# Fewer stored weight operands, fewer partial sums and moved staging in a seven-product MLP

## The chip, the cores and the metric

One core of a Trainium2 chip runs the whole program. The metric is the device time of one execution in microseconds (us). Engines: TensorE (PE, its weight loads PEld), VectorE (DVE), ScalarE (ACT), GpSimd (POOL), and SyncE (SP), which here issues nearly all DMAs.

## The reference, cut to what matters

One layer of a recurrent decoder runs over 2048 prompt tokens and 32 sample tokens. Everything up to the first layer norm is the same before and after; the change lies in the MLP that follows it:

```python
x = layer_norm(ALPHA * x + g1 * mix, ln1_g, ln1_b)
h = x * (1.0 + sc2) + sh2                                   # (2080, 1024)
f = dot(square(relu(dot(h, mlp_w1) + mlp_b1)), mlp_w2) + mlp_b2   # 1024 -> 4096 -> 1024
x = layer_norm(ALPHA * x + g2 * f, ln2_g, ln2_b)
```

All of it is fp32. A product of two fp32 operands is made of three matmuls on fp32r operands: each operand is split into a high part (a copy on ACT) and a low part (operand minus high part, on DVE or POOL), and high*high, high*low and low*high are summed in PSUM.

## The kernel before

**Tiling.** The 2080 tokens are worked on in three groups of 692 to 696 (gidx 0, 1, 2), each in two halves of w = 348 or 346 tokens. The 4096 hidden features are worked on in 16 chunks (c) of 256. Four chunks make a block: four calls of `mlp1` (first matrix) and one call of `mlp2_seven` (second matrix, on two pairs of chunks). Group 2 leaves its last two chunks to plain products.

**Seven products.** Each 2x2 product of blocks takes seven block products (Strassen-Winograd) of the weight operands a11, a12, a22 (plain blocks) and s1 to s4 (sums of blocks) with token operands (b1, b2, t13, t42 in `mlp1`; b11 to b22 and t1 to t4 in `mlp2_seven`). One product is 12 matmuls in `mlp1` and 48 in `mlp2_seven`, so a half block (four `mlp1`, or one `mlp2_seven`) is 336 matmuls.

**PSUM.** In `mlp1`, a11, s2, s3 and a22 add up in one bank (`x`), read by ACT after each step (`s1`, `u2`, `u2` again, then the Relu). s1 (product P5) and s4 (product P3) have banks of their own, and DVE forms `u4` = P5 + u2 from them. Four banks are taken per call from the rotation `M1_BANKS`. In `mlp2_seven`, PRODUCTS says which products go on in the four shared banks `m2x` (True) and which get four banks of their own, and into which quarters of the accumulator `acc` each is added: s1 goes into two quarters, so a call makes 8 x 4 additions to `acc` (on DVE, the first ones of a group on ACT).

**Weights.** In group 0 the raw weights are loaded, combined on DVE, split into operands (`operand`, L763: one 128x1024 tile, high and low half), used, and all stored to DRAM (`W1d`, `W2d`, 512 KB each): 7 per chunk for the first matrix, 14 per pair of chunks for the second. Groups 1 and 2 load those stored operands (`kept`, L773) and split nothing. Group 0's operands live in a ring of 6 buffers (SLOTS), groups 1 and 2 use a ring of 15 (READY); two thirds of group 0's low parts are made by DVE, one third by POOL.

**Staging.** `stage_h` (L704) makes the token operands of a later group: it loads two rows of `Nd`, scales them on ACT, stores, sums them on DVE, and stores again (`Od`). All eight calls, four for group 1 and four for group 2, stand in group 0, after chunks 4 to 11. `conv_h` splits them at the end of a group.

**What sets the order.** A scheduler orders each engine's instructions when the program is built; each engine then runs its list in order. SP's list holds stores (waiting for a split) and loads in one queue. In groups 1 and 2 the layer norm of the group before (`ln2`) runs beside the products.

Of the kernel before, what the change touches and what calls it, by code (L numbers as in the profile page):

```python
# [35 lines left out]
def trunk(ctx: ExitStack, tc: tile.TileContext, *args):  # L36
# [741 lines left out]
    def order_of(gidx, c):  # L778

        if c:  # L780
            return "a11", "a12", "s2", "s1", "s3", "s4", "a22"
        return ("a11", "a12", "s4", "s2", "s1", "s3", "a22") if gidx else ("a11", "s2", "s1", "s3", "a22", "a12", "s4")

    def weights(gidx, c):

# [12 lines left out]
        for key in order_of(gidx, c):  # L798
# [246 lines left out]
    with lpool("p5") as p5_:  # L1045
# [93 lines left out]
        def mlp2_seven(gidx, c0, hids, steps=None):  # L1139
# [3 lines left out]
            pairs = []  # L1143
            for i in range(0, len(hids), 2):
                av = {}
                for key, c, h in () if gidx else (("a11", 0, 0), ("a21", 0, 1), ("a22", 1, 1), ("a12", 1, 0)):
                    t = stage[0](f"q{key}_{gidx}_{c0 + i}").rearrange("p (f d) -> p f d", f=2)
                    r0 = 2 * (c0 + i + c) * P
                    w_load(t, w2[r0:r0 + 2 * P, 512 * h:512 * h + 512].rearrange("(f p) d -> p f d", p=P))
                    av[key] = t  # L1150
# [36 lines left out]
            banks = None  # L1187
            for l, r, grows, to in PRODUCTS:
# [4 lines left out]
                fresh = not (grows and banks)  # L1193
                if not grows:
                    ps = [rot(M2_BANKS, f"m2{l}_{gidx}_{c0}_{b}")[:, :w] for b in range(4)]
                else:
                    if fresh:
                        banks = [ptile([P, 512], X_BANKS[b], f"m2x_{gidx}_{c0}_{b}")[:, :w] for b in range(4)]
                    ps = banks
# [156 lines left out]
        for gidx in range(3):  # L1356
            c0 = 0
            while c0 < NCK - 2 * (gidx == 2):
                hids = []
                for c in range(c0, min(c0 + 4, NCK - 2 * (gidx == 2))):  # L1360
# [525 lines left out]
```

## Time and profile before

| | us |
|---|---|
| three runs | 2157.93, 2162.76, 2165.63 |
| their median | 2162.76 |
| the profiled execution | 2165.93 |
| its span, first to last instruction | 2164.1 |
| PE busy in the span | 2038.4 |
| DVE, ACT, POOL busy | 1426.8, 1006.3, 489.7 |
| moved by DMA | 571.39 MB |

The page has 40 slices of 54 us each: about 14 for what comes ahead of the MLP, then group 0 (some 9 slices, to 1277 us), groups 1 and 2 (to 2107 us) and the end. "PE busy" counts an engine that has an instruction in flight. The views below are the busy times by stretch, the waits of PE's weight loads by what ended them, groups of instructions with mean durations, and a stretch of ACT's timeline.

### The profile page before, as it was taken

The numbers are of one execution on the slowest core, as the hardware profiler recorded it, in microseconds if no ns is written. First come the engines' busy times: TensorE is split into PE (matmuls) and PEld (weight loads), VectorE is DVE, ScalarE is ACT, GpSimd is POOL, SyncE is SP. The second block draws the span as 40 slices with busy tenths as digits, with TensorE's granted clock in tenths as the row PEclk, the third lists the DMA queues.
The fourth block names the chain that finished last, engine by engine and source line by source line (L and its number), as shares of the span: only waits on it lengthen the run. The fifth ranks groups of instructions, "written<-read, shape, count | busy, mean of one in ns | idle before, by whom it ended". The sixth has DMA issues, their size and how long they took to land.

```text
span 2164.1 us, 35479 instructions
## 1 busy us (share of the span) xinstructions
PE 2038.4 (94%) x13055; PEld 1915.4 (89%) x13055; DVE 1426.8 (66%) x2766; ACT 1006.3 (47%) x1923; POOL 489.7 (23%) x327
## 2 busy tenths in 40 slices
PE   7998999989999989889899899999999999999996
PEld 4987888888877789888899889999999999999996
DVE  5677897467887898688797854445444444554476
ACT  3446665546676456554645534333334343333342
POOL 2245323432433322121222401000002000001003
PEclk9999999999999989999999999999999999999998
DMA  9799765453342598999989899888889988898871
GB/s 334 162 267 266 220 192 171 134 149 83 103 110 79 181 325 315 397 341 369 348 325 351 312 365 370 306 282 297 304 293 332 383 302 303 286 310 293 278 271 53
DMA packets 367596, 571.39 MB, mean 264 GB/s; under 512 B 129451, under 2 KB 250703, under 8 KB 367423
## 3 DMA queue, kind: packets, MB, share of 16 engines
q1 hardware_dynamic: 363975, 567.84, 76.8%
q8 instruction: 103, 1.69, 0.3%
q10 hardware_dynamic: 3448, 1.29, 0.2%
q14 instruction: 70, 0.57, 0.1%
HBM read 388.10 MB, written 180.94 MB: 263 GB/s over the span
## 4 chain that ended last, share of the span: by engine, by line
PE 43%; DVE 4%; issue 3%; DMA 2%; POOL 0%; ACT 0%; SPq 0%; POOLq 0%; DVEq 0%; ACTq 0%
PE m1a L1072 15%; PE m2x L1211 11%; PE m1s L1072 6%; PE m2s L1211 6%; PE m2a L1211 3%; PE lt L1297 1%; DVE hw2s L44 1%; DVE acc L44 1%; DMA W1d<-w1s 0%; PE m L1247 0%; PE m L1248 0%; PE m L1249 0%; DVE hid L44 0%; DMA n<-Nd 0%; DVE lb L44 0%
## 5 line engine op out<-in xcount | busy, mean ns | idle before, releaser
L44 POOL TENSOR_TENSOR y<-y,ln_g 128x512 f32<-128x512 f32 (+3 forms) x28 | 37.6, 1360 | 636.7 <-ACT y L65 463.3
L65 ACT ACTIVATE ht<-hid 128x692 fp32r<-128x692 f32 (+1 forms) x92 | 72.1, 783 | 174.1 <-PE m2s L1211 62.8
L65 ACT ACTIVATE hid<-hid 128x346 f32<-128x346 f32 (+1 forms) x240 | 115.9, 491 | 72.3 <-DVE hid L62 63.5
L65 ACT ACTIVATE u<-m1a 128x346 f32<-128x346 f32 (+1 forms) x96 | 43.9, 458 | 188.5 <-PE m1a L1072 181.3
L44 DVE TENSOR_TENSOR lt<-hid,ht 128x692 fp32r<-128x692 f32 (+1 forms) x92 | 87.1, 947 | 64.8 <-ACT ht L65 64.5
L44 DVE TENSOR_TENSOR acc<-m2x,acc 128x346 f32<-128x346 f32 (+1 forms) x168 | 84.3, 513 | 61.4 <-PE m2x L1211 59.9
L62 DVE SCALAR_TENSOR_TENSOR hid<-m1s,vecB,u 128x346 f32<-128x346 f32 (+1 forms) x94 | 53.7, 576 | 97.3 <-ACT u L65 72.6
L44 DVE TENSOR_TENSOR hid<-hid,hid 128x692 f32<-128x692 f32 (+1 forms) x92 | 87.5, 951 | 35.0 <-ACT hid L65 34.9
L1211 PE MATMUL m2x<-ht,hw2s 128*128 128x348 f32 (+1 forms) x392 | 98.9, 329 | 5.3 <-DVE hw2s L44 5.3
L65 ACT ACTIVATE hb<-hid 128x692 fp32r<-128x692 f32 (+1 forms) x69 | 54.0, 784 | 98.7 <-PE m2x L1211 51.6
L44 DVE TENSOR_TENSOR lb<-hid,hb 128x692 fp32r<-128x692 f32 (+1 forms) x69 | 67.2, 974 | 17.6 <-ACT hb L65 17.4
L1211 PEld LDWEIGHTS m2x<-ht,hw2s 128*128 128x128 f32 x392 | 70.3, 194 | 6.6 <-DVE hw2s L44 6.6
L62 DVE SCALAR_TENSOR_TENSOR hid<-m1a,vecB,s 128x346 f32<-128x346 f32 (+1 forms) x48 | 27.6, 576 | 62.5 <-PE m1a L1072 57.5
L44 DVE TENSOR_TENSOR acc<-m2s,acc 128x346 f32<-128x346 f32 (+1 forms) x120 | 56.4, 509 | 13.9 <-PE m2s L1211 13.9
L1211 PE MATMUL m2x<-lt,hw2s 128*128 128x348 f32 (+1 forms) x196 | 63.5, 327 | 0.0
L1072 PE MATMUL m1s<-h2t13h,hw1s 128*128 128x348 f32 (+1 forms) x216 | 57.9, 330 | 4.9 <-DVE x L62 3.7
L44 DVE TENSOR_TENSOR u<-m1s,u 128x346 f32<-128x346 f32 (+1 forms) x48 | 24.8, 516 | 51.9 <-ACT u L65 30.3
L65 ACT ACT_TABLE_LOAD x40 | 51.3, 1283 | 16.0 <-DVE hgb L57 6.5
L1072 PE MATMUL m1a<-h2t42h,hw1a 128*128 128x348 f32 (+1 forms) x192 | 50.9, 328 | 5.8 <-ACT hw1a L65 2.4
L1072 PE MATMUL m1a<-h2t42h,hw1s 128*128 128x348 f32 (+1 forms) x184 | 51.1, 342 | 5.5 <-DVE hw1s L44 4.9
L1072 PE MATMUL m1a<-h2t13h,hw1s 128*128 128x348 f32 (+1 forms) x200 | 52.4, 325 | 2.3 <-ACT hw1s L65 1.7
L956 PE MATMUL op<-hwo,ybh 128*128 128x512 f32 x128 | 51.7, 407 | 2.9 <-ACT ybh L65 2.9
(820 smaller groups left out, 7763.1 us busy)
## 6 DMA issues: line engine op xcount, KB each, us to landing
W1d<-hw1s SPq DMA_DIRECT2D x53, 512.0 KB
W2d<-hw2s SPq DMA_DIRECT2D x53, 512.0 KB
hw1s<-W1d SPq DMA_DIRECT2D x44, 512.0 KB
hw2s<-W2d SPq DMA_DIRECT2D x44, 512.0 KB
lw1s<-W1d SPq DMA_DIRECT2D x42, 512.0 KB
w1s<-W1d SPq DMA_DIRECT2D x42, 512.0 KB
W2d<-hw2a SPq DMA_DIRECT2D x41, 512.0 KB
W1d<-hw1a SPq DMA_DIRECT2D x38, 512.0 KB
```

Source lines behind the costliest of these rows:

```text
L44: return eng.tensor_tensor(out=out, in0=in0, in1=in1, op=op)
L62: return V.scalar_tensor_tensor(out, in0, s, in1, op0, op1)
L65: return S.activation(out, in_, f, **kw).ins
L956: PE.matmul(ac[:w, :], yh[:, kk, o:o + w], wh[:, hs], start=(k == 0), stop=False)
L1072: PE.matmul(ps, x[:, k, :], h[:, k, o:o + w], start=(on is None and k + i == 0), stop=(k == 3 and i == 2), skip_group_check=on is not None)
L1211: PE.matmul(ps[2 * s_ + jj], x[:, f, js], h[:, f, :], start=(fresh and n + f + e == 0), stop=(n == len(pairs) - 1 and f + e == 3), skip_gr ...
L1297: PE.transpose(pt[:w, k * P:k * P + P], src[:, 4 * half + k, :], ident)
```

## The change

1. **mlp1:** s4 (P3) is added up in the bank of s1 (P5), after P5 was read; `u4` and its DVE addition go (one remains in the first chunk of groups 1 and 2, where it serves another purpose). Three banks per call instead of four. Except for the first chunk of groups 1 and 2, all chunks take the order a11, s2, s1, s3, a22, a12, s4.
2. **mlp2_seven:** s1 and s4 share four banks ("y"), a12 gets its own ("o") and comes first. s1 goes into one quarter, so 7 x 4 additions to `acc` are left.
3. **Storing:** group 0 stores s1 to s4 and a11 of the first matrix and s1 to s4 of the second; a12, a22 (first) and a11, a12, a22 (second) are not stored.
4. **Groups 1 and 2:** those plain blocks are loaded raw (one 512 KB load holds two operands) into the ring of 15 and split there, high part on ACT, low part on DVE (kind "c").
5. **Staging:** four calls stay in group 0 (chunks 3, 5, 7, 9, for group 1), four go to group 1 (same chunks, for group 2), with buffers of the ring of 15.

Counted over the program, ACT gets 154 instructions more, DVE 60 more (154 splits, less 46 + 48 additions), SP 157 fewer (80 stores and 77 loads); PE and POOL have as many as before.

```diff
-    W1d = dr.tile([16, 7, P, D], F32, tag="W1d", name="W1d")
-    W2d = dr.tile([8, 7, 2, P, D], F32, tag="W2d", name="W2d")
+    W1d = dr.tile([16, 5, P, D], F32, tag="W1d", name="W1d")
+    W2d = dr.tile([8, 4, 2, P, D], F32, tag="W2d", name="W2d")
...
-    KEYS = ("a11", "a12", "a22", "s1", "s2", "s3", "s4")
+    KEYS = ("s1", "s2", "s3", "s4", "a11")
...
-        low_turn[0] += 1
-        split(hi, lo, v, V if low_turn[0] % 3 else Q)
+        low_turn[0] += kind == "s"
+        split(hi, lo, v, V if kind == "c" or low_turn[0] % 3 else Q)
...
-        if c:
-            return "a11", "a12", "s2", "s1", "s3", "s4", "a22"
-        return ("a11", "a12", "s4", "s2", "s1", "s3", "a22") if gidx else ("a11", "s2", "s1", "s3", "a22", "a12", "s4")
+        if gidx and not c:
+            return "a11", "a12", "s4", "s2", "s1", "s3", "a22"
+        return "a11", "s2", "s1", "s3", "a22", "a12", "s4"
...
         if gidx:
-            return {key: kept(f"w1{key}_{nm}", W1d[c, KEYS.index(key)], 4) for key in order_of(gidx, c)}
+            t = f32(quad("c", f"rw1_{nm}")).rearrange("p (k c) -> p k c", k=4)
+            w_load(t, w1[512:D, c * 256:c * 256 + 256].rearrange("(k p) c -> p k c", p=P))
+            return {key: operand(f"w1{key}_{nm}", t[:, :, P:2 * P] if key == "a22" else t[:, :, 0:P], kind="c")
+                    if key in ("a12", "a22") else kept(f"w1{key}_{nm}", W1d[c, KEYS.index(key)], 4)
+                    for key in order_of(gidx, c)}
...
-            ops[key] = operand(f"w1{key}_{nm}", at[key], W1d[c, KEYS.index(key)])
+            ops[key] = operand(f"w1{key}_{nm}", at[key], W1d[c, KEYS.index(key)] if key in KEYS else None)
...
-        PRODUCTS = (("a11", "b11", True, (0,)), ("s1", "t1", False, (2, 3)), ("a12", "b21", False, (0,)),
-                    ("s2", "t2", True, (2,)), ("s4", "b22", False, (2,)), ("s3", "t3", True, (3,)),
-                    ("a22", "t4", True, (1,)))
+        PRODUCTS = (("a12", "b21", "o", (0,)), ("a11", "b11", "x", (0,)), ("s1", "t1", "y", (3,)),
+                    ("s2", "t2", "x", (2,)), ("s4", "b22", "y", (2,)), ("s3", "t3", "x", (3,)),
+                    ("a22", "t4", "x", (1,)))
...
                     p5_s = prod(key, "t13", 0)
-                    add(V, u4, p5_s, u2)
...
                 elif key == "s3":
                     prod(key, "t13", w, x)
-                    act(u2, x, AF.Copy)
-                    put(1, 1, p5_s, u2)
+                    act(u3, x, AF.Copy)
+                    put(1, 1, p5_s, u3)
                 elif key == "s4":
-                    ps = prod(key, "b2", w)
+                    ps = prod(key, "b2", w, p5_s)
...
-                        put(0, 1, ps, u4)
+                        put(0, 1, ps, u2)
...
+                sums_ = l[0] == "s"
+                if gidx and not sums_:
+                    for n, (nm, av, bv) in enumerate(pairs):
+                        av[l] = raw2(l, c0 + 2 * n, lambda t: f32(quad("c", t)))
...
-                        if gidx:
+                        if gidx and sums_:
                             wh, wl = kept(f"w2{l}{s_}_{nm}", at, 2)
                         else:
-                            wh, wl = operand(f"w2{l}{s_}_{nm}", av[l][:, :, 256 * s_:256 * s_ + 256], at)
+                            wh, wl = operand(f"w2{l}{s_}_{nm}", av[l][:, :, 256 * s_:256 * s_ + 256], at,
+                                             "c" if gidx else "s")
...
-        M1_BANKS, M2_BANKS, X_BANKS = "ADB", "CD", "ABAB"
+        M1_BANKS, M2_BANKS, X_BANKS = "ADB", "CDCD", "ABAB"
...
-        STAGE = range(4, 12)
+        STAGE = range(3, 11, 2)
...
-                    if not gidx and c in STAGE:
-                        i = STAGE.index(c)
-                        stage_h(1 + i // 4, i % 4, raw_tile)
+                    if gidx < 2 and c in STAGE:
+                        stage_h(gidx + 1, STAGE.index(c), (lambda nm: f32(quad("c", nm))) if gidx else raw_tile)
```

Three places in the engines' lists. In them `hw1a11_0_9` is the operand of weight block a11 of group 0, chunk 9, `rw1...` or `qa12...` a raw weight tile, `s1_`, `u2_`, `u3_` copies of the bank `x` (named `m1a11`), `hid` hidden values.

ACT in group 0, around chunk 9's operands, before:

```order
L65 ACTIVATE hw1a11_0_9_11393<-rw10_0_9_11389 128x512
L65 ACTIVATE hid1_0_8_11265<-hid1_0_8_11265 128x348 x2
L65 ACTIVATE hw1a12_0_9_11397<-lrw11_0_9_11391 128x512
L65 ACTIVATE hid0_0_8_11264<-m1a11_0_8_11269,vecB_250 128x348
L65 ACTIVATE nh2_1_1_11537<-nh2_1_1_11537,B1_5870,A1_5869 128x660
L65 ACTIVATE hid0_0_8_11264<-hid0_0_8_11264 128x348
L65 ACTIVATE nh2_2_0_11693<-nh2_2_0_11693,B1_5870,A1_5869 128x660
L65 ACTIVATE s1_0_9_11427<-m1a11_0_9_11430 128x348
L65 ACTIVATE hb11_0_8_11888<-hid0_0_8_11264 128x696
L65 ACTIVATE hw1s2_0_9_11403<-rw10_0_9_11389 128x512
L65 ACTIVATE w1s1_0_9_11407<-rw10_0_9_11389 128x512
L65 ACTIVATE u2_0_9_11428<-m1a11_0_9_11430 128x348
```

and after:

```order
L65 ACTIVATE hw1a11_0_9_11285<-rw10_0_9_11281 128x512
L65 ACTIVATE u2_0_8_11179<-m1a11_0_8_11181 128x348
L65 ACTIVATE hw1s2_0_9_11291<-rw10_0_9_11281 128x512
L65 ACTIVATE hw1s1_0_9_11295<-rw10_0_9_11281 128x512
L65 ACTIVATE u3_0_8_11180<-m1a11_0_8_11181 128x348
L65 ACTIVATE hw1a22_0_9_11304<-lrw11_0_9_11283 128x512
L65 ACTIVATE hid1_0_8_11177<-hid1_0_8_11177 128x348
L65 ACTIVATE s1_0_9_11317<-m1a11_0_9_11320 128x348
```

Before, the splits of chunk 9's s2 and s1 stand behind the copy of chunk 9's first product; after, they stand behind copies of chunk 8's, and two staging instructions (`nh2`) are gone from between.

ACT in group 1, around chunk 5, after:

```order
L65 ACTIVATE u2_1_5_14747<-m1a11_1_5_14749 128x346
L65 ACTIVATE y5_00_256_14990<-y5_00_256_14990,AB_5872,mods_78 128x92 x8
L65 ACTIVATE u3_1_5_14748<-m1a11_1_5_14749 128x346
L65 ACTIVATE hw1a22_1_7_15051<-lrw1_1_7_15041 128x512
L65 ACTIVATE hw1a12_1_7_15054<-lrw1_1_7_15041 128x512
L65 ACTIVATE hid1_1_5_14745<-hid1_1_5_14745 128x346
L65 ACTIVATE s1_1_6_14887<-m1a11_1_6_14890 128x346
```

Two splits of chunk 7 are new there, between two copies of chunk 5's and chunk 6's banks; before, no split stands in group 1's list outside `conv_h` and the hidden values' own.

SP in group 1, the loads of chunk 4's first-matrix weights, after:

```order
L757 DMA lrw1_1_4_14552<-in_mlp_w1_dram 128x4x256
L757 DMA hw1a11_1_4_14554<-W1d_71 128x1024
L757 DMA hw1s2_1_4_14556<-W1d_71 128x1024
L757 DMA hw1s1_1_4_14558<-W1d_71 128x1024
L757 DMA hw1s3_1_4_14560<-W1d_71 128x1024
L757 DMA lw1s4_1_4_14568<-W1d_71 128x1024
```

These are six loads where seven stood; the first is raw and has to be split into two operands.

## Rows read from the trace of the kernel before

**Rows 1.** The page: busy time, granted clock and DMA in 40 slices.

```profile
PE 2038.4 (94%) x13055; PEld 1915.4 (89%) x13055; DVE 1426.8 (66%) x2766; ACT 1006.3 (47%) x1923; POOL 489.7 (23%) x327
...
PEclk9999999999999989999999999999999999999998
DMA  9799765453342598999989899888889988898871
```

**Rows 2.** Busy time by stretch: group 0's half blocks, then groups 1 and 2.

```profile
core 0: us, PE busy (x) PEld busy (x) DVE busy (x) ACT busy (x) POOL busy (x), PEclk, DMA share, GB/s
756.00:826.00 70.00, 62.55 (x354) 59.57 (x353) 63.68 (x117) 36.44 (x72) 16.37 (x10) 0.90 0.90 324
826.00:879.30 53.30, 52.62 (x328) 51.73 (x326) 45.25 (x61) 32.95 (x59) 14.06 (x10) 1.00 0.89 335
879.30:950.00 70.70, 60.65 (x349) 56.45 (x349) 48.16 (x72) 38.22 (x73) 14.49 (x11) 0.98 1.01 380
950.00:1009.50 59.50, 56.99 (x338) 53.11 (x337) 56.60 (x88) 27.22 (x44) 12.74 (x9) 1.00 0.91 339
1009.50:1079.00 69.50, 59.84 (x338) 54.65 (x338) 46.37 (x79) 35.84 (x70) 12.96 (x10) 0.98 0.96 360
1079.00:1138.40 59.40, 56.11 (x338) 55.00 (x337) 56.18 (x82) 25.35 (x42) 14.92 (x10) 0.97 0.88 331
1138.40:1195.00 56.60, 53.63 (x329) 51.81 (x328) 41.43 (x60) 30.24 (x61) 11.94 (x9) 1.00 0.93 343
1195.00:1277.20 82.20, 70.89 (x407) 68.49 (x406) 64.93 (x81) 36.89 (x63) 29.63 (x17) 0.94 0.91 334
...
1323.00:2100.00 777.00, 776.58 (x4914) 774.79 (x4913) 379.80 (x736) 280.08 (x535) 71.39 (x54) 1.00 0.88 309
```

**Rows 3.** PE's weight loads, 879.3 to 1138.4 us: waited for, us, times, longest.

```profile
PEld m1a L1072 <- ACT hw1a L65: 6.7, 6, 1.4
PEld m1a L1072 <- DVE hw1s L44: 6.0, 4, 2.7
...
PEld m1a L1072 <- ACT u L65: 2.6, 3, 0.9
```

**Rows 4.** The same view, 1195 to 1277.2 us, then 1323 to 2100 us.

```profile
PEld m2s L1211 <- DVE hw2s L44: 5.5, 3, 2.7
...
PEld lt L1297 <- DVE y L62: 0.7, 1, 0.7
```

**Rows 5.** ACT's timeline in group 0: start, us, instruction, idle before and releaser.

```profile
1011.59 0.46 ACT L65 ACTIVATE s<-m1a 128x348 f32<-128x348 f32 x1 [7.21 <-PE m1a L1072]
1011.94 0.62 ACT L65 ACTIVATE hw1a<-lrw 128x512 fp32r<-128x512 f32 x1
1012.46 0.62 ACT L65 ACTIVATE hw1s<-rw 128x512 fp32r<-128x512 f32 x1
1019.31 0.46 ACT L65 ACTIVATE u<-m1a 128x348 f32<-128x348 f32 x1 [6.22 <-PE m1a L1072]
1019.66 0.62 ACT L65 ACTIVATE hw1s<-rw 128x512 fp32r<-128x512 f32 x1
```

**Rows 6.** DVE groups by shape, 879.3 to 1138.4 us: count, busy, mean ns, idle before.

```profile
L44 DVE TENSOR_TENSOR acc<-m2s,acc 128x348 f32<-128x348 f32 x24 | 11.3, 509 | 1.3 <-PE m2s L1211 1.3
L44 DVE TENSOR_TENSOR nh<-nh 128x346 f32<-128x346 f32 x15 | 9.8, 651 | 0.1
L44 DVE TENSOR_TENSOR nh<-nh,nh 128x346 f32<-128x346 f32 x14 | 7.6, 540 | 1.1 <-ACT nh L65 0.9
L44 DVE TENSOR_TENSOR hw1a<-lrw,hw1a 128x512 fp32r<-128x512 f32 x9 | 6.2, 686 | 2.2 <-ACT hw1a L65 2.2
L44 DVE TENSOR_TENSOR u<-m1s,u 128x348 f32<-128x348 f32 x8 | 4.2, 520 | 3.8 <-PE m1s L1072 2.5 <-ACT hw1a L65 1.3
```

**Rows 7.** DMAs: the staging's stores (880 to 1195 us); all packets of 879.3 to 1009.5 us.

```profile
Od<-nh SPq DMA_DIRECT2D x22, 346.0 KB
...
DMA packets 18738, 47.04 MB, mean 361 GB/s; under 512 B 1588, under 2 KB 6771, under 8 KB 18729
```

More of the change, by code (lines that the diff above doesn't have):

```diff
@@ L761, in both, with operand @@
         return [t[:, 512 * i:512 * i + 512].rearrange("p (a b) -> p a b", a=n) for i in range(2)]
-    def operand(nm, v, keep=None):
-        t = quad("s", nm)
+    def operand(nm, v, keep=None, kind="s"):
+        t = quad(kind, nm)
         hi, lo = both(t, v.shape[1])
-        low_turn[0] += 1
-        split(hi, lo, v, V if low_turn[0] % 3 else Q)
+        low_turn[0] += kind == "s"
+        split(hi, lo, v, V if kind == "c" or low_turn[0] % 3 else Q)
         if keep is not None:
@@ L1092, in put @@
                 square(v, SQA[2 * f + q])
-            s1, u2, u4 = vt("s1"), vt("u2"), vt("u4")
+            s1, u2, u3 = vt("s1"), vt("u2"), vt("u3")
             v01, v10 = hid[1][:, 0, :], hid[0][:, 1, :]
@@ L1107, in mlp1 @@
                     p5_s = prod(key, "t13", 0)
-                    add(V, u4, p5_s, u2)
                     if gidx and not c:
-                        add(V, v01, v01, u4)
+                        add(V, u2, p5_s, u2)
+                        add(V, v01, v01, u2)
                         square(v01, SQA[1])
@@ L1143, in mlp2_seven, with raw2 @@
             pairs = []
-            for i in range(0, len(hids), 2):
[L1145 to L1150, printed above, removed]
+            def raw2(key, cc, tile_):
+                c, h = {"a11": (0, 0), "a21": (0, 1), "a22": (1, 1), "a12": (1, 0)}[key]
+                t = tile_(f"q{key}_{gidx}_{cc}").rearrange("p (f d) -> p f d", f=2)
+                r0 = 2 * (cc + c) * P
+                w_load(t, w2[r0:r0 + 2 * P, 512 * h:512 * h + 512].rearrange("(f p) d -> p f d", p=P))
+                return t
+            for i in range(0, len(hids), 2):
+                av = {key: raw2(key, c0 + i, stage[0]) for key in (() if gidx else ("a11", "a21", "a22", "a12"))}
                 pairs.append((f"{gidx}_{c0 + i}", av, {"b11": hids[i][0], "b12": hids[i][1], "b21": hids[i + 1][0],
@@ L1186, in mlp2_seven @@
             taken = [c0 > 0] * 4
-            banks = None
-            for l, r, grows, to in PRODUCTS:
+            banks = {}
+            for l, r, total, to in PRODUCTS:
                 rs = []
@@ L1192, in mlp2_seven @@
                     rs.append(part(f"{r}_{nm}", bv[r]))
[L1193 to L1199, printed above, removed]
+                fresh = total not in banks
+                if fresh:
+                    banks[total] = [ptile([P, 512], (X_BANKS if total == "x" else M2_BANKS)[b],
+                                          f"m2{total}_{gidx}_{c0}_{b}")[:, :w] for b in range(4)]
+                ps = banks[total]
+                sums_ = l[0] == "s"
+                if gidx and not sums_:
+                    for n, (nm, av, bv) in enumerate(pairs):
+                        av[l] = raw2(l, c0 + 2 * n, lambda t: f32(quad("c", t)))
                 for s_ in range(2):
                     for n, ((nm, av, bv), (hh, hl)) in enumerate(zip(pairs, rs)):
-                        at = W2d[c0 // 2 + n, KEYS.index(l), s_]
-                        if gidx:
+                        at = W2d[c0 // 2 + n, KEYS.index(l), s_] if sums_ else None
+                        if gidx and sums_:
                             wh, wl = kept(f"w2{l}{s_}_{nm}", at, 2)
                         else:
-                            wh, wl = operand(f"w2{l}{s_}_{nm}", av[l][:, :, 256 * s_:256 * s_ + 256], at)
+                            wh, wl = operand(f"w2{l}{s_}_{nm}", av[l][:, :, 256 * s_:256 * s_ + 256], at,
+                                             "c" if gidx else "s")
                         for jj in range(2):
```

## The prediction, made before the result was known

> **What bounds the kernel now.** I read the page first, then a table of stretches, then the waits of PE's weight loads. The page [rows 1] shows PE busy 94% of the span and DMA near 9 tenths in most slices of the MLP, so any gain must come from a stretch in which PE waits. I cut the MLP at its half blocks [rows 2]: group 0's are A (756 to 826), B, C, D, E, F, G and H (1195 to 1277.2), in turn four `mlp1` calls and one `mlp2_seven` of 336 matmuls each. B takes 53.3 us with PE busy 52.6 of them; that is my measure of a half block at PE's own pace. Groups 1 and 2 run at that pace: in 1323 to 2100 PE is busy 776.58 of 777 us at full clock, DVE only 379.8 and ACT 280.1 [rows 2], and a weight load hardly ever waits there (the one wait shown is 0.7 us) [rows 4]. Nothing can be won in them, only lost.
>
> Group 0 is different. C to F take 70.7 + 59.5 + 69.5 + 59.4 = 259.1 us against 4 x 53.3 = 213.2, an excess of 45.9. G has 3.3. H has 82.2 less 48 early matmuls of group 1 (7.6 us), 74.6, an excess of 21.3. A has 16.7, but it is the start, beside the end of the stage ahead. PE's loads in C to F wait for operands being split [rows 3]; the 19 such rows, of which the first two stand there, add up to 35 us. Two things lie behind. DMA is full: 1.01 in C, 0.96 in E [rows 2], and C + D move 47.04 MB [rows 7], in 130.2 us. And DVE is nearly full in the second-matrix halves: 56.6 of 59.5 in D. ACT also works its list in order: a split behind the copy `u` waited 6.22 us with it for PE, and PE next needed that split [rows 5].
>
> **Part 1, staging.** All eight staging calls fall in C to F. B and G, without them but with the same stores, are the pair to compare: 259.1 - 2 x (53.3 + 56.6) = 39.3 us, so 4.9 us per call. One call moves five pieces of 346 KB and one of half that [rows 7], 1.95 MB; at C's 380 GB/s [rows 2] that is 5.1 us. Price and transfer time agree, which makes DMA the bound there. Four calls leave group 0: -19.6 us. In group 1 a call adds 2 x 0.65 + 2 x 0.54 us to DVE [rows 6] and its bytes to a DMA that gets 20% lighter; PE has cover of half of DVE there, so I cost it at 0 (bounds: 0 and the same 4.9 each, 19.6). Each call's six DMAs also stand in SP's list in front of weight loads, and the stores wait for ACT and DVE; what hides that is the ring of 15, which holds about 15 x 1.9 = 28 us of products ahead (12 matmuls of 53.3 / 336 us each take 1.9), now some 24 us since 66 instead of 56 tiles pass through it per block.
>
> **Part 2, stores not made.** Per block 8 + 12 = 20 stores of 512 KB go, 10.5 MB; with two calls of staging less (3.9 MB), C + D move 47.0 - 14.4 = 32.6 MB. At the pace of two half blocks that is 306 GB/s, and groups 1 and 2 run at 309 with PE full [rows 2]. E + F go from 44.7 (69.5 us at 360 GB/s and 59.4 at 331 [rows 2]) to 44.7 - 10.5 - 5.9 = 28.3 MB. So DMA stops being the bound, and the four calls that stay lose what made them dear. Next is DVE. C + D hold 104.8 us of it; four `u` additions of 0.52, four `acc` additions of 0.51 and two calls of 2.4 go [rows 6], leaving 95.9 of 106.6 us, 90%. E + F, with three calls less, come to 91, 86%. B ran at PE's pace with DVE at 85% [rows 2]. So most of the excess should go, not all: I leave 12 of the 45.9 us in C to F (bounds: 0, and 45.9 - 19.6 = 26.3 if only the moved staging counts). With part 1 that is -34 us. In the lists, the splits of a chunk now stand a chunk ahead of the copies that they stood behind, which fits. [...]
>
> **Part 3, the sums.** The additions in C to F are counted above. G loses four of `u`: -1 us. H is bound by DVE (64.9 us, and its waits are for DVE's splits [rows 4]; clock 0.94); it loses four `acc` additions (2 us), its first two products need no sums of weights, its stores shrink: -4 (bounds 0 and its excess, 21.3). A gets one staging call: +1 (0 to 4.9). P3 in P5's bank makes PE wait for the reading of P5 (0.58 us on DVE) only if nothing lies between; a22 and a12, 24 matmuls or 3.8 us, do: 0. Without that cover it is 0.6 us x 48 = 28.
>
> **Part 4, the splits in groups 1 and 2.** 2 x 32 in `mlp1` and 6 for each of 15 pairs: 154. Each is 0.62 us of ACT [rows 5] and 0.69 of DVE [rows 6]: 95 and 106 us in 830, which takes ACT from 36 to about 47% and DVE from 49 to 58% (after the additions that go). Throughput covers that; order may not. From below: 0, as the rows have half of each engine idle. From above: group 0's excess in C to F, 45.9 us for its 112 operands, 0.41 each, so 63 us. I take 4, near the lower end, since three of group 0's conditions (6 buffers, stores, full DMA) are missing, and the first chunks of group 1 still follow H.
>
> **Sum.** -34 - 1 - 4 + 1 + 4 = -34 us on 2165.93, the profiled execution: 2131.9. It lay 3.2 above the median of the runs, so 2128.7; I say **2129**.
>
> **The rivals.** *Full recovery*: with DMA free, C to F and G go to PE's pace (-49), H loses 15, A 3: -67, 2096. For it: B; the lists. Against: DVE at 90% in C + D and no new room in H. *Only a little*: the order, not DMA, makes the waits. Then C to F win about half of the DVE time that goes (8.9 + 11.3, so 10) and the rest 1: 2152. For it: PE's waits name ACT and DVE, none a DMA [rows 3]; against it: 4.9 us per staging call equals its transfer, and B, with the same order of work, is at PE's pace. *Slower*: ACT and DVE in groups 1 and 2. A split waits in ACT's list behind a copy that waits for PE, as in [rows 5], and PE then waits for its operand; or a split stands ahead of a copy that frees the bank. At 0.41 us per split this costs 63 instead of 4: 2188. It decides from (34 + 4) / 154 = 0.25 us per split on. For it: 154 new places, in a ring that reaches 24 us instead of 28. Against it: the new splits in the list of chunk 5 belong to chunk 7, two chunks or some 27 us ahead, and both engines are half idle. [...] Taken as every high copy of 0.62 us holding up PE, it would add 95 us: 2220. *No effect*: the bytes go, but raw tiles in shorter rows cost what the stored ones did, and the gain and part 4 balance: 2163.
>
> **How the numbers follow.** Forecast (gain 22 to 50) 0.55; full recovery 0.14; only a little 0.12; no effect 0.07; slower 0.12. A measurement of this kernel tells 0.3% (6.5 us) from no change: faster 0.81, same 0.07, slower 0.12. The range leaves out the slower cases and no effect and the far end of full recovery: from 2094 to 2156.
>
> **What would show it.** Right: stores cut to 36 per block; C to F together 215 to 235 us with DMA at 0.8 or below; H about 78; groups 1 and 2 still 107 us per block with PE without gaps, ACT near 47%. Part 1 is wrong if the stretch with two staging calls is as long as C was; part 2 is wrong if DMA falls and PE still waits for ACT or DVE splits in C and E; part 4 is wrong if PE's loads after 1280 us wait for `hw1a`, `w2a` operands or the clock falls there. The whole is wrong if PE, now ahead, meets DVE in D and H, so that these grow by what C and E win.

## The result, and the profile after

The changed kernel runs in 2137.39 us (median; 2134.06 to 2149.31), the kernel before, beside it on the same chip, in 2159.18 (2157.93 to 2165.63): a ratio of 0.9899, 95% interval 0.9873 to 0.9926. It is faster by 22 us (1%) where 34 were forecast, and inside the range. The profiled executions lie 28 us apart (2137.69 and 2165.93); 6.6 of these fall ahead of the MLP, in code that the change doesn't touch, so 21.7 remain, as by the medians.

The page of the changed kernel, to be read beside [rows 1]: busy time, granted clock and DMA.

```profile
PE 2022.4 (95%) x13055; PEld 1908.0 (89%) x13055; DVE 1497.1 (70%) x2826; ACT 1090.1 (51%) x2077; POOL 509.6 (24%) x327
...
PEclk9999999999999989999999999999999999999998
DMA  9799765452433485958576888786778967685761
```

Its stretches, with the columns of [rows 2]: group 0 as a whole, in it C to F and H; groups 1 and 2.

```profile
749.80:1223.80 474.00, 447.43 (x2726) 435.93 (x2725) 395.86 (x569) 259.61 (x471) 141.37 (x83) 0.99 0.75 272
873.00:1099.30 226.30, 219.89 (x1354) 216.71 (x1353) 189.37 (x271) 123.30 (x223) 60.56 (x38) 0.99 0.74 273
1152.00:1224.00 72.00, 62.95 (x370) 60.01 (x369) 65.81 (x81) 35.64 (x59) 29.92 (x15) 0.98 0.79 278
1223.80:2077.10 853.30, 839.52 (x5262) 833.14 (x5261) 495.52 (x904) 394.25 (x753) 84.13 (x59) 1.00 0.76 264
```

The same two long stretches of the kernel before.

```profile
756.40:1277.30 520.90, 472.99 (x2765) 450.46 (x2763) 422.28 (x634) 263.15 (x482) 127.11 (x83) 0.97 0.92 344
1277.30:2107.20 829.90, 827.68 (x5233) 825.12 (x5231) 404.57 (x782) 306.13 (x587) 78.16 (x58) 1.00 0.88 310
```

Group 0 did what was forecast: C to F take 226 us for 259, with DMA at 0.74 for 0.94. Groups 1 and 2, in which PE had worked without gaps, now have 14 us in which PE is idle. The waits of PE's weight loads there (us in all, times, longest; a load's wait is longer than the gap that it leaves between matmuls, 2.33 us for 2.04 at 1383.67: before that gap each load starts 0.16 us ahead of its matmul) name one cause above all:

```profile
PEld m1a L1078 <- ACT u L65: 15.6, 14, 2.6
PEld lt L1310 <- issue: 2.3, 1, 2.3
```

`m1a` is the bank `x` of `mlp1`, `u` the copies u2 and u3 that ACT makes of it. Before a product may add to the bank, the copy of what stands there must be done. Of the 13.8 us in which PE is idle, 11.5 end with such a copy, and 2.1 are one stop at the transposes `lt` of the second layer norm. These are not waits for split operands.

For all that follows, the stretches are made comparable: PE issues some of group 1's matmuls before group 0 ends (61 before, 21 after), some 10 of group 0's ahead of its stretch, and some of the last `mlp1` among the plain part (12 before, 24 after); each is put back at 0.16 us. So counted, the MLP has two stretches: **group 0**, 512.8 us before and 472.2 after, and **groups 1 and 2**, 841.6 before and 860.5 after. The plain part behind them is 55 us in both. -40.6 + 18.9 = -21.7: that is the whole change. (The expectations of e1 to e8 speak of the stretch as the trace has it, 853 us in the change; those of e9 to e11 of the counted one, 861.)

### The profile page after: what moved, and what is told of

It reads as the page before. It is cut to its first block, busy times and chain, and to the rows that moved or that the text cites. A ratio compares the mean times of both kernels' runs of the same rounds, so it can differ in the third digit from the quotient of the medians.

```text
span 2135.8 us, 35452 instructions
## 1 busy us (share of the span) xinstructions
PE 2022.4 (95%) x13055; PEld 1908.0 (89%) x13055; DVE 1497.1 (70%) x2826; ACT 1090.1 (51%) x2077; POOL 509.6 (24%) x327
## 4 chain that ended last, share of the span: by engine, by line
PE 64%; DVE 18%; DMA 6%; ACT 5%; issue 4%; POOL 2%; SPq 1%; ACTq 0%; DVEq 0%; POOLq 0%
PE m1a L1078 19%; PE m2x L1224 14%; PE m1s L1078 7%; PE m2y L1224 6%; PE m2o L1224 3%; DVE xc L62 1%; PE pa L185 1%; PE accg L373 1%; PE accg L374 1%; PE accg L375 1%; DVE gi L347 1%; PE accb L374 1%; DMA qa<-in_mlp_w_dram 1%; PE accb L375 1%; PE accb L373 1%
## 5 line engine op out<-in xcount | busy, mean ns | idle before, releaser
L1224 PE MATMUL m2x<-ht,hw2s 128*128 128x348 f32 (+1 forms) x352 | 87.4, 322 | 2.2 <-DVE hw2s L44 1.5
L44 DVE TENSOR_TENSOR lb<-hid,hb 128x692 fp32r<-128x692 f32 (+1 forms) x69 | 61.7, 916 | 7.9 <-ACT hb L65 7.8
L1224 PEld LDWEIGHTS m2x<-ht,hw2s 128*128 128x128 f32 x352 | 61.6, 188 | 3.0 <-DVE hw2s L44 1.7
L65 ACT ACTIVATE hb<-hid 128x692 fp32r<-128x692 f32 (+1 forms) x69 | 52.6, 778 | 21.7 <-PE m2x L1224 13.3
L1224 PE MATMUL m2x<-lt,hw2s 128*128 128x348 f32 (+1 forms) x176 | 55.9, 324 | 2.3 <-DVE lt L44 2.2
L1224 PE MATMUL m2x<-ht,w2s 128*128 128x346 f32 (+1 forms) x216 | 55.8, 321 | 0.0
L1078 PE MATMUL m1a<-h2b1h,hw1a 128*128 128x348 f32 (+1 forms) x208 | 54.8, 323 | 0.8 <-ACT hw1a L65 0.5
L62 DVE SCALAR_TENSOR_TENSOR E<-E,et 128x16 f32<-128x16 f32 (+3 forms) x128 | 46.1, 399 | 10.5 <-ACT et L65 10.4
L1078 PE MATMUL m1s<-h2t13h,hw1s 128*128 128x348 f32 (+1 forms) x192 | 50.1, 323 | 3.5 <-DVE x L62 3.4
L963 PE MATMUL op<-hwo,ybl 128*128 128x512 f32 x128 | 51.5, 404 | 1.2 <-DVE ybl L44 1.2
L1078 PE MATMUL m1a<-h2t42h,hw1s 128*128 128x346 f32 (+1 forms) x200 | 51.9, 322 | 0.0
```

Source lines behind the costliest of these rows:

```text
L44: return eng.tensor_tensor(out=out, in0=in0, in1=in1, op=op)
L62: return V.scalar_tensor_tensor(out, in0, s, in1, op0, op1)
L65: return S.activation(out, in_, f, **kw).ins
L963: PE.matmul(ac[:w, :], yl[:, kk, o:o + w], wh[:, hs], start=False, stop=False)
L1078: PE.matmul(ps, x[:, k, :], h[:, k, o:o + w], start=(on is None and k + i == 0), stop=(k == 3 and i == 2), skip_group_check=on is not None)
L1224: PE.matmul(ps[2 * s_ + jj], x[:, f, js], h[:, f, :], start=(fresh and n + f + e == 0), stop=(n == len(pairs) - 1 and f + e == 3), skip_gr ...
```

## The experiments

The change has three parts that can stand alone: the sums in shared banks with their order (S), the plain blocks not stored but split anew (P), and the moved staging (M). The table has every kernel that ran, with the time against the kernel before on the same chip, and the two stretches as counted above. PE's early matmuls and the position of a boundary leave about 1 us of doubt in a stretch, which is that of one profiled execution; the median of a run has about 3.

| kernel | ratio to before, 95% interval | group 0, us | groups 1 and 2, us |
|---|---|---|---|
| before | 1 | 512.8 | 841.6 |
| M alone (e8) | 0.9935 [0.9916, 0.9955] | 493.9 | 842.6 |
| P alone (e7) | 0.9836 [0.9819, 0.9853] | 475.9 | 841.2 |
| P + M (e2) | 0.9780 [0.9760, 0.9800] | 464.1 | 840.4 |
| S alone (e4) | 1.0109 [1.0093, 1.0125] | 518.1 | 860.2 |
| S + P (e3) | 0.9907 [0.9892, 0.9923] | 481.9 | 852.1 |
| S + P + M, the change | 0.9899 [0.9873, 0.9926] | 472.2 | 860.5 |
| P + M, S in mlp1 only (e6) | 0.9882 [0.9865, 0.9898] | 467.0 | 858.8 |
| the same, mlp1's old order (e11) | 0.9896 [0.9879, 0.9912] | 464.0 | 863.7 |
| P + M, only mlp1's new order (e10) | 0.9773 [0.9759, 0.9788] | 465.0 | 838.7 |
| the change, mlp1's sums of before in groups 1, 2 (e1) | 0.9927 [0.9911, 0.9943] | 473.4 | 860.8 |
| the change, a11 x b11 first in mlp2 (e5) | 0.9860 [0.9841, 0.9880] | 465.7 | 855.3 |
| both of these (e9) | 0.9831 [0.9817, 0.9846] | 465.1 | 849.2 |

### Is it the sums, the splits or the staging that groups 1 and 2 pay for?

**e1**: the changed kernel, with `mlp1` of before in groups 1 and 2.

```
+        if gidx and c:
+            return "a11", "a12", "s2", "s1", "s3", "s4", "a22"
...
+                    if alone:
+                        u4 = u3
+                        add(V, u4, p5_s, u2)
...
-                    ps = prod(key, "b2", w, p5_s)
+                    ps = prod(key, "b2", w, None if alone else p5_s)
```

> The changed kernel, with the sums of mlp1 in groups 1 and 2 as they were before (P3 in a bank of its own, the sum P5 + u2 made on DVE, the old order of products). Theory (lost cover): the steps that add up in bank x stand next to each other at the end of each block of four chunks, and PE waits there for the copy u on ACT; 13.6 us of PE waits after 1224 us and 6.8 us at half clock cost groups 1 and 2 about 15 us. Then these waits fall to 3 us or less, the stretch from the last m2x of group 0 to the first plain m falls from 853 to 838 to 842 us, and the time from 2137 to about 2123. Rival (splits): the 154 new splits hold up ACT and DVE, the copies u with them. Then the stretch stays at 850 or more and the time at 2137. Rival (staging in group 1): likewise 2137, the blocks 1 and 2 of group 1 stay at 111 to 113 us.

Measured: 2145.48 against 2163.4, groups 1 and 2 at 860.8. Nothing came back, but the waits changed their name. PE's loads in groups 1 and 2:

```profile
PEld m2o L1231 <- ACT hb L65: 8.4, 8, 2.3
PEld m1a L1080 <- ACT u L65: 7.2, 5, 3.5
```

`m2o` is the first product of `mlp2`, a12 x b21, which needs hidden values of the second chunk of each pair. The number in the expectation failed, and with it the picture that `mlp1` alone pays.

**e2**: S undone in both matrices (banks, order, the sum u4); the splits and the staging stay as changed.

```
-        return "a11", "s2", "s1", "s3", "a22", "a12", "s4"
+        if c:
+            return "a11", "a12", "s2", "s1", "s3", "s4", "a22"
...
-                    ps = prod(key, "b2", w, p5_s)
+                    ps = prod(key, "b2", w)
...
-                        put(0, 1, ps, u2)
+                        put(0, 1, ps, u4)
...
-        PRODUCTS = (("a12", "b21", "o", (0,)), ("a11", "b11", "x", (0,)), ("s1", "t1", "y", (3,)),
+        PRODUCTS = (("a11", "b11", True, (0,)), ("s1", "t1", False, (2, 3)), ("a12", "b21", False, (0,)),
...
-        M1_BANKS, M2_BANKS, X_BANKS = "ADB", "CDCD", "ABAB"
+        M1_BANKS, M2_BANKS, X_BANKS = "ADB", "CD", "ABAB"
```

> The changed kernel, with the sums as before in all groups and in both matrices (P5 and P3 in banks of their own, u4 and the second addition into acc on DVE, the old order); plain blocks split anew and the moved staging stay. Theory (lost cover): groups 1 and 2 win back 12 to 15 us; group 0 loses the relief of DVE, 8.9 us of DVE time in C + D and 11 in E + F, of which a part shows: 0 to 10 us. Together 2122 to 2133, half blocks C to F 226 to 236 us. Rival (splits in groups 1 and 2): nothing is won there, 2137 to 2147. Rival (the relief of DVE carries group 0's gain, not the bytes): C to F go back by 15 us or more, to 241 or over.

Measured: 2112.87 against 2163.4. Its group 0 and its groups 1 and 2, then the one wait for `u` that is left in the latter:

```profile
753.50:1218.30 464.80, 444.36 (x2719) 436.59 (x2718) 417.26 (x601) 257.46 (x472) 136.11 (x83) 0.98 0.78 276
1218.30:2054.50 836.20, 835.28 (x5280) 833.11 (x5280) 517.29 (x966) 392.89 (x749) 80.49 (x58) 1.00 0.79 269
```

```profile
PEld m1a L1078 <- ACT u L65: 0.9, 1, 0.9
```

PE is busy 835.3 of 836.2 us with all the new splits in place and DVE busier than in the change. So the splits are not the cause, the sums are; and group 0 gains too, where the relief of DVE should have been lost. This kernel beats both.

**e4**: S alone, on the kernel before: the edit of e2 with + and - exchanged.

> The kernel before, with only the sums changed (P5 and P3 in one bank, the three totals of mlp2, the order of products); all seven operands stored, eight staging calls in group 0. Theory (lost cover): groups 1 and 2 lose 10 to 16 us, with PE waiting for the copy u at the ends of blocks; group 0 gains little, since DMA stays full: C to F 250 to 259 us, H 4 less. Together 2158 to 2172, no gain. Rival (splits): groups 1 and 2 lose nothing, as there are no splits in them: their stretch is 838 us, and the time 2145 to 2158. Rival (DVE, not DMA, made the waits of group 0): C to F fall to 240 or under.

Measured: 2184.59 against 2163.4, 21 us slower, more than expected. Groups 1 and 2 lose 18.6 us without one new split in them. In group 0, C to F grow from 259 to 266 us, and beside the waits for splits there are now waits of bank `x` for its copies, 10.4 us by these two rows (879 to 1145 us; [rows 3] had 2.6):

```profile
PEld m1a L1072 <- ACT u L65: 6.1, 9, 0.8
...
PEld m1a L1072 <- ACT s L65: 4.3, 5, 1.2
```

**e3**: all eight staging calls in group 0 again.

```
-        STAGE = range(3, 11, 2)
+        STAGE = range(4, 12)
...
-                    if gidx < 2 and c in STAGE:
-                        stage_h(gidx + 1, STAGE.index(c), ...)
+                    if not gidx and c in STAGE:
+                        i = STAGE.index(c)
+                        stage_h(1 + i // 4, i % 4, raw_tile)
```

> The changed kernel, with all eight staging calls in group 0 again, as before. Part 1 of the prediction priced a call at 4.9 us while DMA is full; without the stores it is not full (0.91 of it in C, 0.62 in D), so the price may have gone: theory (bytes): C to F rise from 226 by 4 to 12 us, the time to 2141 to 2149; if each call still costs 4.9, C to F rise by 19.6 to 246 and the time to 2157. Rival (staging in group 1 is what groups 1 and 2 lost): the stretch from the last m2x of group 0 to the first plain m falls from 853 to about 838, blocks 1 and 2 of group 1 (113, 111 us) to 108, and the time stays near 2137 or falls. Under lost cover that stretch stays at 850 to 853.

Measured: 2141.41 against 2163.4. C to F grow by 10 us to 236, as expected for bytes; groups 1 and 2 win 8.4 (852.1 for 860.5). So the moved staging does cost there, but only with the new sums: without them M costs 1.0 (e8) and -0.8 us (e2 against e7). Nor do the sums need it: S alone loses 18.6 us there with no staging in group 1, S + P 10.9. The trace of the change shows one case, in group 1 at 1376 us: the last matmul of PE's step s2 on bank `x`, DVE's list, ACT's, and PE's next step, s3.

```profile
1379.42 0.32 PE L1078 MATMUL m1a<-h2t42h,lw1s 128*128 128x346 f32 x1
...
1379.52 0.52 DVE L44 TENSOR_TENSOR hnh<-hnh,hnh 128x346 f32<-128x346 f32 x1 [2.60 <-DMA Od<-hnh]
1380.07 0.52 DVE L44 TENSOR_TENSOR hnh<-hnh 128x346 f32<-128x346 f32 x1
1380.51 0.57 DVE L62 SCALAR_TENSOR_TENSOR hid<-m1s,vecB,u 128x346 f32<-128x346 f32 x1
...
1381.11 0.49 ACT L65 ACTIVATE hid<-hid 128x346 f32<-128x346 f32 x1 [4.08 <-DVE hid L62]
1381.74 0.63 ACT L65 ACTIVATE w2a<-qa 128x512 fp32r<-128x512 f32 x1
1382.28 0.61 ACT L65 ACTIVATE hw2a<-qa 128x512 fp32r<-128x512 f32 x1
1382.80 0.47 ACT L65 ACTIVATE hid<-hid 128x346 f32<-128x346 f32 x1
1383.18 0.44 ACT L65 ACTIVATE u<-m1a 128x346 f32<-128x346 f32 x1
...
1383.67 0.61 PE L1078 MATMUL m1a<-h2t13h,lw1s 128*128 128x346 f32 x1 [2.04 <-ACT u L65]
```

The staging's DVE instruction waits 2.60 us for the store of the tile that it overwrites; the reading of P5 (`hid<-m1s`) stands behind it; ACT's square waits 4.08 us for that; two splits of the plain blocks and `u` stand behind the square; PE waits 2.04 us for `u`. What `u` copies was ready when s2 ended, at 1379.7, and ACT stood idle until 1381.11: the order of its list held `u` back. The clock follows:

```profile
1383.80:1387.20 3.40, 3.40 (x12) 3.20 (x12) 1.98 (x3) 1.15 (x2) 0.00 (x0) 0.51 0.45 129
```

That is the lower level, 0.51 in this stretch and 1.00 ahead of it and behind it: 12 matmuls in 3.4 us where 21 would fit. It comes again at 1475.9, behind a wait that is not for `u`: DVE stands 8.60 us for a load of the second norm's rows, and PE 2.08 us for its transposes.

```profile
1473.56 2.19 DVE L62 SCALAR_TENSOR_TENSOR y<-n,AG,y 128x128 f32<-128x128 f32 x8 [8.60 <-DMA n<-Nd]
1474.01 1.86 PE L1310 MATMUL lt<-ident,y 128*128 128x128 f32 x7 [2.08 <-DVE y L62]
...
1475.90:1479.30 3.40, 3.40 (x14) 3.34 (x13) 2.44 (x5) 1.29 (x4) 0.00 (x0) 0.50 1.03 412
```

Before, the granted clock stays at the upper level, 1.00, from 1236.5 us to the plain part. PE's idle time there has grown from 2.2 to 13.8 us; with these 2 x 1.7 us that makes 15.0 of the 18.9 us, and the rest is not placed. S + P (e3) has neither of the two stops: its loads wait at most 1.4 us for `u` and 0.2 for `y`, and its clock is 1.00 over the whole stretch, a mean in which two falls of 3.4 us would not show (the change's mean is 1.00 as well). With the clock the two stops are 7.5 of the 8.4 us; that e3 has no such fall is taken for this sum, not shown. That the late load behind the second comes from the staging is not shown.

### Which part of the sums?

**e5**: the changed kernel, with one line edited.

```
-        PRODUCTS = (("a12", "b21", "o", (0,)), ("a11", "b11", "x", (0,)), ("s1", ...
+        PRODUCTS = (("a11", "b11", "x", (0,)), ("a12", "b21", "o", (0,)), ("s1", ...
```

> The changed kernel with one edit: in the order of mlp2's products, a11 x b11 stands ahead of a12 x b21 again, as before; the sums stay in the new banks, mlp1 is untouched. b11 comes from the first chunk of a pair, b21 from the second, so the first product of mlp2 is ready earlier and can stand between the last steps of mlp1 on bank x. Theory (lost cover, of which mlp2's first product is the main part): PE's waits for u and for hb at the ends of blocks fall from 11 to 4 us or less, the stretch from the last m2x of group 0 to the first plain m falls from 853 to 838 to 845 us, the time from 2137 to 2122 to 2130. Rival (the shared bank in mlp1 and its order are what costs): the waits for u stay, the stretch stays at 850, the time at 2137.

Measured: 2131.76 against 2161.14. Group 0 gets 6.5 us back of the 8.1 that S costs there on P + M (472.2 against 464.1), groups 1 and 2 get 5.2 of 20. By size it stands between theory and rival. Nine waits for `u` are left:

```profile
PEld m1a L1078 <- ACT u L65: 10.3, 9, 2.8
```

**e6**: the changed kernel with the sums of `mlp2` as before (the last two pieces of e2's edit); **e11**: that, with `mlp1`'s old order too; **e10**: P + M with `mlp1`'s new order and nothing else of S. The edit of e11 is

```
-        if gidx and not c:
-            return "a11", "a12", "s4", "s2", "s1", "s3", "a22"
-        return "a11", "s2", "s1", "s3", "a22", "a12", "s4"
+        if c:
+            return "a11", "a12", "s2", "s1", "s3", "s4", "a22"
+        return ("a11", "a12", "s4", "s2", "s1", "s3", "a22") if gidx else ("a11", "s2", "s1", "s3", "a22", "a12", "s4")
```

and that of e10 the reverse, on e2.

> The changed kernel with the sums of mlp2 as before in all groups (a11 x b11 first, products of their own in banks C and D, the second addition of s1 into acc); mlp1 keeps the new sums (P5 and P3 in one bank) and the new order. Theory (mlp2's first product is the main part of the lost cover): stretch of groups 1 and 2 836 to 843 us, time 2113 to 2125, near the 2112.9 without any of the new sums. Rival (mlp1's shared bank and order cost most): stretch 848 to 853, time 2130 to 2140.

> The version without the new sums, with the new order of mlp1's products alone: P3 keeps a bank of its own, u4 is made on DVE, mlp2 is as before. Theory (the shared bank: s4 may not start before s3 is done and P5 read, so it no longer fills the time in which u is copied): the order alone costs little, groups 1 and 2 840 to 846 us, time 2113 to 2119. Rival (the order itself, with a12 and s4 taken from between the steps on bank x): groups 1 and 2 at 853 to 859, time 2126 to 2135.

> The version with mlp2's sums as before, mlp1's P5 and P3 in one bank, but mlp1's old order of products (a12 and s4 between the steps on bank x). Theory (the shared bank binds s4): the waits for u at the ends of blocks stay, groups 1 and 2 at 850 to 859 us, time 2125 to 2136, near the 2134.9 with the new order. Rival (the order): groups 1 and 2 back at 840 to 846, time 2113 to 2119.

Measured: e6 2134.94 against 2161.14, e10 2113.98 and e11 2140.18 against 2162.5. For e6 the rival held. The new order without the bank costs nothing: e10's groups 1 and 2 take 838.7 us, a little less than its theory had, and `u` is not among the waits. The bank with the old order costs 23 us (863.7), a little more than its theory had. So in `mlp1` it is the shared bank and not the order. This holds with `mlp2`'s sums as before; beside the new ones, a bank of its own for P3 brings nothing alone (e1) and 6.1 us where a11 x b11 is first (e9 against e5). Groups 1 and 2 of e10, then e11's waits:

```profile
1222.50:2056.10 833.60, 833.46 (x5275) 832.10 (x5274) 512.22 (x965) 392.94 (x749) 83.28 (x58) 1.00 0.78 269
```

```profile
PEld m1a L1078 <- ACT u L65: 10.8, 7, 4.3
```

The longest but one of e11's stops for `u`, on PE and ACT:

```profile
1797.91 0.32 PE L1078 MATMUL m1a<-h2t13h,lw1s 128*128 128x346 f32 x1
1798.90 1.88 ACT L65 ACTIVATE y<-y,AB,mods 128x90 f32<-128x90 f32 x5 [5.55 <-DMA y<-Cd]
1800.69 0.44 ACT L65 ACTIVATE u<-m1a 128x346 f32<-128x346 f32 x1
...
1801.18 0.65 PE L1078 MATMUL m1a<-h2t42h,lw1a 128*128 128x346 f32 x1 [2.95 <-ACT u L65]
```

ACT waits 5.55 us for rows of the second norm to be loaded, `u` stands behind them, and PE waits 2.95 between the last matmul of s3 and the first of a22, where its list has nothing else. P + M has such stops on ACT too, and PE doesn't notice them; this is its group of these instructions in groups 1 and 2 (count, busy us, mean ns, idle before them and what ended it):

```profile
L65 ACT ACTIVATE y<-y,AB,mods 128x128 f32<-128x128 f32 (+2 forms) x96 | 37.5, 472 | 30.0 <-DMA y<-Cd 30.0
```

The difference is in PE's list. At that place (group 2, chunk 5) P + M has 42 matmuls between s3 and a22, e10 has 35, e11 none. At the end of the first block of group 1, between s2 and the next step on bank `x`, s3, stand:

| kernel | matmuls between s2 and s3 | of these s4 | between s3 and a22 |
|---|---|---|---|
| before | 23 | 11 | 23 |
| e2, P + M | 30 | 12 | 23 |
| e10, new order | 25 | 12 | 23 |
| the change | 18 | 0 | 0 |
| e1 | 23 | 12 | 13 |
| e6 | 16 | 0 | 23 |
| e11 | 23 | 0 | 23 |

With a bank of its own, s4 needs nothing that comes late: in before, P + M and e10 its 12 matmuls (1.9 us) stand in these two places at the ends of all seven full blocks. In P5's bank it may start only when s3 is done, u3 copied and P5 read, so it stands last.

What that does to the list shows over all of groups 1 and 2. Bank `x` has 96 places where one step follows another (three per chunk, 32 chunks); counted in PE's timeline, this stands between the two steps:

| kernel | fewest matmuls | places with none | PE idle at these, us |
|---|---|---|---|
| P + M | 13 | 0 | 0 |
| e10 | 21 | 0 | 0 |
| the change | 0 | 12 | 9.3 |
| S alone | 0 | 14 | 12.0 |
| S + P | 0 | 11 | 7.0 |
| e6 | 0 | 3 | 3.5 |
| e11 | 0 | 4 | 8.1 |

In the change and the four versions below it PE stops at every place with none, and waits for no `u` where 18 or more stand. So `mlp2`'s matmuls cover a copy too, as at e11's block ends; what costs are the places left bare, and in e6 and e11 also waits of `mlp2`'s own matmuls for `hid`, `hb`, `ht` and `lb`. Cover is no guarantee: e1 waits 1.7 and P + M 0.6 us for `u` once behind 23 matmuls. That it is the place of s4 that leaves them bare, and not the rotation of the banks, which changes with it (three banks per call for four), is argued from the list, not tried by itself.

**e9**: e1 and e5 together.

> The changed kernel with both repairs of the two runs ahead together: in groups 1 and 2 the sums of mlp1 as before (P3 in a bank of its own), and in all groups a11 x b11 ahead of a12 x b21 in mlp2; mlp2's new totals stay, and in group 0 mlp1's new sums. Theory (at a block's end PE needs products that wait for nothing; each half of the new sums takes some away, and with either half the waits come): both back, so groups 1 and 2 return from 861 us (early matmuls counted in) to 841 to 846, group 0 stays near 466, and the time is 2113 to 2120. Rival (the totals of mlp2, held in banks over several products, cost by themselves): groups 1 and 2 stay at 853 or over, time 2127 or more.

Measured: 2126.21 against 2162.5, groups 1 and 2 at 849.2: between theory and rival. Of the 8.8 us above P + M, 5.4 are two gaps of PE in the last two chunks; the rest is not placed. The longer gap, on ACT:

```profile
2062.61 1.15 ACT L65 ACTIVATE lw<-rw 128x512 fp32r<-128x512 f32 x2 [0.65 <-DMA rw<-in_mlp_w_dram]
2063.67 0.53 ACT L65 ACTIVATE hid<-m1a,vecB 128x346 f32<-128x346 f32 x1
2064.10 0.62 ACT L65 ACTIVATE lw<-rw 128x512 fp32r<-128x512 f32 x1
2064.62 0.48 ACT L65 ACTIVATE hid<-hid 128x346 f32<-128x346 f32 x1
2065.00 0.44 ACT L65 ACTIVATE u<-m1a 128x346 f32<-128x346 f32 x1
```

`u` stands behind splits for the plain part, which wait for raw weights. Elsewhere e9 has lost the waits but for 1.9 us, so there the totals that `mlp2` holds in banks cost little by themselves. In the last two chunks every kernel with either half of S has a gap of over 1 us (1.1 to 4.3), and the five without (before, e2, e7, e8, e10) have none. e9 has only `mlp2`'s half in these chunks, so that half is enough to bring the gap; by which step is not shown.

### What do the other two parts bring alone?

**e7**: P alone, on the kernel before.

```
-    KEYS = ("a11", "a12", "a22", "s1", "s2", "s3", "s4")
+    KEYS = ("s1", "s2", "s3", "s4", "a11")
...
-            ops[key] = operand(f"w1{key}_{nm}", at[key], W1d[c, KEYS.index(key)])
+            ops[key] = operand(f"w1{key}_{nm}", at[key], W1d[c, KEYS.index(key)] if key in KEYS else None)
...
+                if gidx and not sums_:
+                    for n, (nm, av, bv) in enumerate(pairs):
+                        av[l] = raw2(l, c0 + 2 * n, lambda t: f32(quad("c", t)))
```

**e8**: M alone, on the kernel before: e3's edit with + and - exchanged.

> The kernel before with only the plain blocks not stored and split anew in groups 1 and 2; sums as before, all eight staging calls in group 0. Theory (bytes and DVE): most of the 50 us of the version without the new sums is here; with the calls back in group 0, C to F are 4 to 12 us longer than its 220, 224 to 232, and groups 1 and 2 stay at 836 to 838: time 2117 to 2125 against 2163 before. Rival (the moved staging carries half the gain, 19.6 us): 2131 to 2135. Rival (the splits in groups 1 and 2 cost 0.41 us each): 63 us more there, time 2175 or more.

> The kernel before with only the staging moved: four calls stay in group 0, four go to group 1. Part 1 of the prediction: 4.9 us per call while DMA is full, nothing in group 1: C to F 259 less 19.6 = 239 us, the time 2163 less 19 = 2144. Rival (a call costs about 2.5 us, as in the version without stores): C to F 249, the time 2153. Rival (the wait goes on to other places, or group 1 pays it back): within 6 us of before, 2157 to 2165.

Measured: e7 2126.06 against 2161.14, e8 2147.14 against 2161.14. C to F take 234.9 and 237.8 us, so they win 24.2 and 21.3 of the 259.1: e8 near what was expected, e7 a little less (its C to F were expected at 224 to 232, and its time is 1 us over its range). Groups 1 and 2 of e7:

```profile
1232.10:2069.10 837.00, 835.58 (x5281) 833.23 (x5280) 504.72 (x936) 387.75 (x743) 83.51 (x58) 1.00 0.76 260
```

With 154 splits more and DVE at 505 us for 405 before, PE is idle 1.4 us.

## Why the prediction came out as it did

**What bounds the kernel** was read rightly: group 0 waits, groups 1 and 2 have nothing to give. All the gain is in group 0, all the loss in the other two.

**Part 1** holds at its price. M alone wins 21.3 us in C to F where 19.6 were forecast. By the plan five calls leave C to F and one comes to A, so the price is better read over all of group 0: 18.9 us for four calls, 4.7 each for the 4.9 forecast. Once the stores are gone too, it is 11.8 us (e7 less e2), some 3 each. In group 1 a call costs next to nothing, as said (1.0 and -0.8 us for all four). With the new sums they cost 8.4, in part through a wait that the working didn't list: it counted what a call adds to DVE's busy time, not that DVE stands still in its list for the staging's store (2.60 us), with the reading of P5 queued behind it.

**Part 2** was right in kind and too small. P alone wins 36.9 us in group 0, 24.2 of it in C to F and some 13 in the other half blocks. Of these 24.2 the working left 14.4 for it and the sums together, and 5 in G and H. P + M win 48.7 us in group 0, 39.5 of the excess of 45.9 in C to F: more than the forecast, less than the full recovery (-67) that was a rival. The working had no term for the clock: in group 0 it was granted at the lower level (0.50) for 34 us before and 10 after, which is at most 12 of the 40.6 us (less where PE would have waited anyway).

**Part 3** is the step that failed. It was forecast to help (the additions saved on DVE counted into C to F, -1 in G, part of the -4 in H) with the shared bank at 0. S costs 5.3 us in group 0 alone, 6.0 on P and 8.1 on P + M, and 18.6, 10.9 and 20.1 us in groups 1 and 2. The prediction asked what lies between P5's reading and the product that overwrites it, found a22 and a12, and was right: no wait of `m1s` for that reading shows in groups 1 and 2 of the change. It didn't ask where a12 and s4 had been taken from. They had been the products that stood between the steps on bank `x`, and the shared bank, which binds s4 to the end of its chunk, costs 20 us (e6 against e10, both in the new order) to 23 (e11 against e2, both in the old) with `mlp2`'s sums as before. That the price of 28 us without cover comes near this is luck: it was worked out for another wait, at another bank. The second half of the miss is `mlp2`'s first product: a12 x b21 needs the second chunk's hidden values, and its new place got no term for groups 1 and 2. That half alone costs as much (e1, 860.8 for P + M's 840.4), so the two don't add up.

**Part 4** is right at its lower bound: 154 splits cost -0.4 us on the kernel before (841.2 against 841.6) and -2.2 on M; in the change ACT is busy 46% and DVE 58% there, as forecast (47 and 58). The rival that ended on the slower side, splits blocking ACT's list, is no cause by itself. The second form of its mechanism did come: a copy `u` waits behind splits (at 1383.18 above), and PE notices it because nothing covers it any more. ACT and DVE take their lists in order there, as the 2.60 us on DVE and the 4.08 and 5.55 us on ACT above show.

**The sum.** Group 0: -40.6 for a forecast of -38 (-34 - 1 - 4 + 1), where P + M brought 10.7 more than that and S took 8.1. Groups 1 and 2: +18.9 for +4. That makes -21.7 for -34. That the time lies inside the range by so much is in part luck, since errors of both signs met: P + M won 10.7 us more in group 0 than was forecast, S lost 8.1 there, and groups 1 and 2 lost 14.9 more than the 4 they were given. The base, 2162.76, was the median of three runs; of six it is 2159.18, so 2137 lies nearer to the forecast 2129 than the gains do.

**What would show it**: C to F at 226 lie in 215 to 235, with DMA at 0.74; H at 72.0 less 21 early matmuls (3.4) is 68.6 where 78 with 48 of them, so about 70 without, was forecast. The trace of before has 61 early ones and not 48, so H went from 72.4 to 68.6, which is the 4 us of the forecast. Groups 1 and 2 did not stay at 107 us per block, and PE's loads there wait for `u`, not for `hw1a` or `w2a` as the sign of a wrong part 4 would have had it. Its other sign, that the clock falls there, came (0.51 at 1383.8, 0.50 at 1475.9), but part 4 is not what it tells of: P + M has all the splits and neither of the two stops (its loads wait 0.9 us at most), at a mean clock of 1.00.

## What to carry to other kernels

When a product is put into a bank that is already in use, ask of each product that this binds: what did it cover where it stood? Here s4's 12 matmuls, 1.9 us per chunk, stood where the bank was copied (0.45 us a copy); sharing the bank cost 20 to 23 us in all, while the additions that it saves are on DVE, which was busy 49% of the time there. In PE's list, look for two steps on one bank with nothing between. Of a change in several parts run the parts alone: here two of the three brought 50 us, and the third took 29 of it back.

## What the runs showed of the hardware that was not expected

A stretch in which ACT and DVE are half idle can still make PE wait. In groups 1 and 2 of the change ACT is busy 46% and DVE 58% of the time, and single stops of 2.60 (DVE, for a store) with 4.08 (ACT, for DVE), and of 5.55 us (ACT, for a load, in e11), pass through the lists to PE.

The granted clock fell after single gaps, and the length of a gap alone does not tell when. In groups 1 and 2 of the change it was granted at the lower level (0.51 and 0.50) for 3.4 us after each of two gaps, of 2.04 and 2.08 us, although PE was busy 839 of 853 us. After a gap of 2.35 us in the same run (to 2075.0), one of 1.33 us (to 1502.7) and nine of 0.55 us it stayed at 1.00.
